# 256-token stages of a two-block transformer kernel: the high and low parts of the activations as one 512-column matmul

## The chip, the cores and the metric

The kernel runs on one core of a Trainium2 chip, in one launch. The metric is device time in microseconds (us). Weights come from HBM on every execution and are used once.

The core's engines have in-order queues and meet through semaphores: PE (matrix multiply), DVE (vector), ACT (scalar, with activation functions), POOL (GpSimd) and SP (here it only issues DMAs). PEld in the profile is PE loading its stationary operand, which overlaps the matmul before.

## The reference, cut to what matters

Two transformer blocks of width 1024 on 256 tokens. The second block runs two layers; it puts 16 meta tokens in front, so its first layer works on 272 tokens, and its second layer again on the 256.

```python
y = jnp.square(jax.nn.relu(h2 @ w_mlp_in[l])) @ w_mlp_out[l]      # block 1: 1024 -> 4096 -> 1024
x = x + gate2[:, None, :] * y
...
def swiglu(h, w_gate, w_up, w_down):                               # block 2: 1024 -> 2816 -> 1024
    return (jax.nn.silu(h @ w_gate) * (h @ w_up)) @ w_down
...
for l in range(DEPTH_2):                                           # two layers, two swiglu each
    h = h + 0.5 * swiglu(rmsnorm_2(h, ffn1_norm[l]), ffn1_w_gate[l], ffn1_w_up[l], ffn1_w_down[l])
    ...
    h = h + 0.5 * swiglu(rmsnorm_2(h, ffn2_norm[l]), ffn2_w_gate[l], ffn2_w_up[l], ffn2_w_down[l])
```

Everything is float32.

## The kernel before

**Splitting.** PE works on `float32r`, a shortened float. So that nothing is lost, every operand is split into a high part and a rest: `hi` is the value rounded by ACT, `lo = value - hi` is made by DVE. A product is then three matmuls, written by `mm3` (lines 116 to 121): high weight with high activation, high weight with low activation, low weight with high activation, all summed into the same columns of a PSUM bank. This text calls the three a triple. Each of the three loads its own stationary weight tile of 128x128.

**Weights.** A weight block is 1 MB, 128 partitions by 2048 values. `ld` (line 82) issues its DMA into one of 3 `raw` buffers, and splits it in two halves of 1024 columns: ACT writes `whi` (line 103), DVE writes `wlo` (line 104). There are 4 `whi` and 4 `wlo` buffers, so two blocks. A half of `whi` can be written when PE has used the half two blocks before it. Half a and half b below are the two halves of one block.

**Activations.** Features lie on partitions, tokens on columns. High and low parts have tiles of their own: `ah` and `al` for the MLP's hidden activations, `gh` and `gl` for those of the FFNs, `yh` and `yl` for the normed input.

**The stages.** `proj` (line 243) walks over weight blocks; one step is one block, two PSUM banks and 16 triples (8 feature tiles of the input by two output tiles). In an FFN, step f gives the gate and the up values of hidden tile f, and `evac` (in `ffn`) takes them out: DVE multiplies the gate sums by the norm's row `R` (line 698), ACT applies Silu (699), DVE multiplies the up sums by `R` (701), POOL multiplies both (702), ACT makes the high part (192) and DVE the low part (193). The first steps wait for `R`, so that their evacuations come together when it lands. `down` (line 627) walks over the second matrix; its evacuation is `devac` (712) or, in block 1, `mlp_out_evac` (648).

The stages on 256 tokens that the change speaks of are the MLP's second matrix in block 1 (4 x 4 blocks) and the two FFNs of the second layer, here called the first and the last 256-token FFN (22 gate/up blocks and 12 down blocks each). In the first of them the projection to the shared latent keys (`latent`) stands behind step 4, two small pieces behind steps 6 and 8.

**Order.** The Tile framework orders the instructions of each engine ahead of time, and each engine then takes its list strictly in order.

Of the kernel before, what the change touches and what calls it, by code (L numbers as in the profile page):

```python
# [18 lines left out]
S = 256  # L19
# [10 lines left out]
# columns of the packed per-feature vectors  # L30
# [15 lines left out]
def net(ctx, tc, d):  # L46
# [35 lines left out]
    def ld(src, n, sub=1024, spare=False, pool=False, cut=False, steps=None, after=((), ())):  # L82
        """parts of a weight block; with steps, the part behind the first is left to a call of what is put there"""
        raw = wp.tile([128, 2048], F32, tag="raw", name=nm("raw"), bufs=3)
        for a, b in ((0, sub), (sub, n)) if cut else ((0, n),):
            with behind(order[:1]):
                i = nc.sync.dma_start(raw[:, a:b], src[:, a:b])
            if order:
                order[:1] = [i]
        parts = []  # L90
        if spare:
            bh, bl = blk([128, 2048], F32R), blk([128, 2048], F32R)

        def part(a):
            m = min(sub, n - a)
            if spare:
                hi, lo = bh[:, a:a + m], bl[:, a:a + m]
            else:
                hi = wp.tile([128, 1024], F32R, tag="whi", name=nm("whi"), bufs=4)
                lo = wp.tile([128, 1024], F32R, tag="wlo", name=nm("wlo"), bufs=4)  # L100
            e = G if pool and a else V
            with behind(after[a > 0]):
                i = A.activation(hi[:, :m], raw[:, a:a + m], AF.Copy)  # L103
                e.tensor_tensor(lo[:, :m], raw[:, a:a + m], hi[:, :m].bitcast(F32), op=OP.subtract)  # L104
            if order and not a:
                order[1:] = [i]
            parts.append((hi, lo))

        for a in range(0, n, sub):
            if a and steps is not None:  # L110
                steps.append(lambda a=a: part(a))
            else:
                part(a)
        return parts

    def mm3(out, w, c0, xh, xl, start, stop, m=128):
        """out += (whi + wlo).T (xhi + xlo), the weights stationary."""
# [3 lines left out]
        TE.matmul(out, lo[:, c0:c0 + m], xh, start=False, stop=stop, skip_group_check=True)  # L121

# [88 lines left out]
    def sumsq_late(parts, src, f, n, sumsq=sumsq):  # L211
        """as sumsq, the last two tiles on their own: their squares are ready sooner."""
# [10 lines left out]
    def proj(src, evac, nj, n, yh, yl, first=2, hooks=(), at={}, orders=(range(0, 6), range(6, KD)), spare=(),  # L223
             after={}):
        """two feature tiles by step. The first steps take the tiles of y in the given order, with what is ready
        first in front; the hooks go behind each part of the order and behind the steps that follow, and only
        then the first sums are used. at[j] goes behind step j."""
# [10 lines left out]
        def mms(pp, w, ks, tiles=(0, 1)):  # L238
            for k in ks:
                for i in tiles:  # L240
                    mm3(pp[i][:, 0:n], w[k // 4], (k % 4) * 256 + i * 128, yh[:, k, :], yl[:, k, :],
                        k == 0, k == KD - 1)
# [50 lines left out]
    def ada(ch, t0, t1, early=False):  # L293
        """feature tiles t0, t1 of the modulation: a row of ada_w.T per partition, times silu(c), summed."""
# [12 lines left out]
    def ada_rest(n, early=False):  # L307
        """n more chunks: gate1, scale2, shift2, gate2."""
# [22 lines left out]
    # position bias with its masks, as a Toeplitz table  # L331
# [50 lines left out]
    # q feature tiles (tokens back to front within each half), then k  # L382
# [25 lines left out]
    def scores(fam, half):  # L408
# [22 lines left out]
        if fam == 0:  # L431
            # heads i, i+4, i+1, i+5 of the sinks
# [24 lines left out]
    def values(fam, heads, Sb, rd, mid):  # L457
        PTs, po = [], []

        def tr(j):  # L460
# [7 lines left out]
            PTs.append(work([128, 384], "PT", bufs=3))  # L468
# [74 lines left out]
    # branches, merge  # L543
# [19 lines left out]
    # out projection, residual; y = x1 * g2 * (1 + scale2), with shift2 as two more columns  # L563
# [27 lines left out]
    # MLP  # L591
    ah = [blk([128, 8, S], F32R) for _ in range(4)]
    al = [blk([128, 8, S], F32R) for _ in range(4)]

    def mlp_evac(f, p):
# [17 lines left out]
    # MLP out, residual; final norm of block 1 and first norm of block 2 both applied late  # L613
# [14 lines left out]
    def down(src, kcs, evac, n, ah, al, before=None):  # L628
        for dp in range(4):
# [3 lines left out]
            for c, (k0, nk) in enumerate(kcs):  # L633
                w = ld(src(dp, c), nk * 256)
                for kk in range(nk):
                    k = k0 + kk
                    for i in range(2):
                        mm3(pp[i][:, 0:n], w[kk // 4], (kk % 4) * 256 + i * 128, ah[k // 8][:, k % 8, :],
                            al[k // 8][:, k % 8, :], k == 0, k == kcs[-1][0] + kcs[-1][1] - 1)
# [15 lines left out]
    down(lambda dp, c: d["mlp_out"][dp * 4 + c], [(8 * c, 8) for c in range(4)], mlp_out_evac, S, ah, al,  # L655
# [17 lines left out]
    def rms_of(get, tiles, n):  # L673
        """hooks that leave the norm of y's tokens in a row."""
# [14 lines left out]
    def ffn(idx, yh, yl, rms, h, n, c0, post, kv=False, before=None, **kw):  # L689
        """h[:, c0:] + half of the swiglu of y; post(f, h_f) for each feature tile of the sum."""  # L690
        gh = [blk([128, nk, n], F32R) for _, nk in FC]
        gl = [blk([128, nk, n], F32R) for _, nk in FC]
        hooks, rc = rms
        c1 = T - n if kv else 0

        def evac(f, pg, pu):
            g = work([128, PADW], "t")[:, :n]
# [37 lines left out]
    # layer 0  # L735
# [25 lines left out]
    def window(g, w, l0, l1, E):  # L761
        """sums over 2, 4, 8, 16 tokens back"""
# [54 lines left out]
    # shared keys and values  # L817
# [76 lines left out]
    # layer 1  # L894
# [93 lines left out]
    def mla_values(b, Pb, rd):  # L988
        PTs = []
        po = ps()  # L990
        for j in range(2):
# [7 lines left out]
            PT = work([128, 384], "PT", bufs=3)  # L999
# [18 lines left out]
    p3 = post_y(y3, ("ffn2_norm", 8), S)  # L1018
# [20 lines left out]
    # the queries' norms and the scale go with the exponentials  # L1039
# [61 lines left out]
def _layout(i):  # L1101
# [15 lines left out]
    def pairs(w):  # L1117
        """[K, F] -> [F / 256, 128, (K / 128) * 256]"""
# [3 lines left out]
    def tiles(w, c):  # L1122
        """[K, F] -> [128, (F / c) * (K / 128) * c]"""
# [78 lines left out]
```

## Time and profile before

| | |
|---|---|
| median of 3 runs | 1280.71 us (1280.71 to 1281.14) |
| span of the profiled execution, first to last instruction | 1279.0 us |
| what lies around the span, median less span | 1.7 us |
| PE busy | 1240.4 us, 97% of the span |
| DVE busy | 855.1 us, 67% |
| ACT busy | 611.3 us, 48% |
| POOL busy | 363.7 us, 28% |
| granted PE clock, mean | 0.993 of 2.4 GHz |

The busy shares are means over stages with different limits. A row of a timeline gives the start in us from the span's start and the duration of an instruction; recorded durations of one engine overlap a little, since instructions are pipelined, so the pace of an engine is read from starts. The bracket at the end of a row is the idle time ahead of it and what ended it.

### The profile page before, as it was taken

Reading aid. Unit: us, or ns where it says so; the run is one execution under the profiler, and the core shown is the slowest. Engines: PE = TensorE matmul, PEld = TensorE weight load, DVE = VectorE, ACT = ScalarE, POOL = GpSimd, SP = SyncE. Lnnn points to the kernel's source line nnn. Section 1 sums busy time; section 2 is a strip of 40 time slices with the busy share of each in tenths; the row PEclk is TensorE's granted clock in tenths of the full one; section 3 lists DMA queues with packets and bytes.
Section 4 is the critical chain, followed back from the end, with each engine's and each line's share of the span. In section 5 each row is a group of like instructions: output and inputs, shape, how many; then the busy total and the mean of one; then the engine's idle time right before and its main releaser. Section 6 shows DMA issues by size and latency. Waiting matters only on the chain.

```text
span 1279.0 us, 24155 instructions
## 1 busy us (share of the span) xinstructions
PE 1240.4 (97%) x9908; PEld 1213.6 (95%) x9908; DVE 855.1 (67%) x1322; ACT 611.3 (48%) x971; POOL 363.7 (28%) x351
## 2 busy tenths in 40 slices
PE   6999999999999999998899999999999999999997
PEld 4988999999999999998899999999999977999997
DVE  7978778887755766566866666666656577666543
ACT  3366445665444544443444444454444454544442
POOL 4333135331325222223222212222222235222221
PEclk9999999999999999999999999999999999999999
DMA  8957864556664554451455455455555423555551
GB/s 326 331 187 285 307 226 169 198 176 253 210 219 165 168 188 173 159 206 65 165 182 181 165 178 168 166 199 170 193 181 182 132 100 129 183 183 189 169 185 53
DMA packets 37057, 238.63 MB, mean 187 GB/s; under 512 B 4242, under 2 KB 6738, under 8 KB 11731
## 3 DMA queue, kind: packets, MB, share of 16 engines
q1 hardware_dynamic: 36946, 237.10, 52.9%
q8 instruction: 77, 1.26, 0.4%
q14 instruction: 34, 0.27, 0.1%
HBM read 236.01 MB, written 1.07 MB: 185 GB/s over the span
## 4 chain that ended last, share of the span: by engine, by line
PE 86%; DVE 7%; issue 3%; POOL 2%; ACT 2%; POOLq 0%; DVEq 0%; ACTq 0%
PE ps L121 27%; PE ps L120 27%; PE ps L119 27%; DVE wlo L104 2%; DVE blk L302 1%; DVE blk L189 1%; POOL blk L341 1%; DVE blk L768 1%; POOL t L561 1%; PE ps L477 1%; PE ps L150 1%; PE ps L467 0%; ACT whi L103 0%; PE ps L175 0%; PE ps L523 0%
## 5 line engine op out<-in xcount | busy, mean ns | idle before, releaser
L121 PE MATMUL ps<-blk,wlo 128*128 128x256 f32 (+2 forms) x3080 | 878.3, 286 | 9.6 <-DVE wlo L104 6.2
L120 PE MATMUL ps<-blk,whi 128*128 128x256 f32 (+2 forms) x3080 | 879.4, 286 | 2.9 <-DVE blk L361 1.8
L119 PE MATMUL ps<-blk,whi 128*128 128x256 f32 (+2 forms) x3080 | 871.1, 286 | 7.6 <-ACT blk L188 4.3
L104 DVE TENSOR_TENSOR wlo<-raw,whi 128x1024 fp32r<-128x1024 f32 (+2 forms) x395 | 485.8, 1233 | 248.0 <-ACT whi L103 247.5
L121 PEld LDWEIGHTS ps<-blk,wlo 128*128 128x128 f32 x3080 | 588.3, 191 | 11.8 <-DVE wlo L104 7.4
L119 PEld LDWEIGHTS ps<-blk,whi 128*128 128x128 f32 x3080 | 585.8, 192 | 10.0 <-ACT blk L188 4.5
L120 PEld LDWEIGHTS ps<-blk,whi 128*128 128x128 f32 x3080 | 588.6, 191 | 3.8 <-DVE blk L361 2.3
L103 ACT ACTIVATE whi<-raw 128x1024 fp32r<-128x1024 f32 (+3 forms) x403 | 412.5, 1030 | 364.4 <-PE ps L120 339.3
L702 POOL TENSOR_TENSOR u<-u,t 128x272 f32<-128x272 f32 (+1 forms) x88 | 117.5, 1336 | 349.0 <-ACT t L699 344.7
L192 ACT ACTIVATE blk<-u 128x272 fp32r<-128x272 f32 (+1 forms) x88 | 37.2, 424 | 129.6 <-POOL u L702 129.6
L193 DVE TENSOR_TENSOR blk<-u,blk 128x272 fp32r<-128x272 f32 (+1 forms) x88 | 39.1, 446 | 83.5 <-ACT blk L192 83.5
L200 POOL TENSOR_TENSOR sq<-blk 128x256 f32<-128x256 f32 (+1 forms) x45 | 36.7, 817 | 129.1 <-DVE blk L712 124.8
L201 POOL TENSOR_TENSOR ss<-ss,sq 128x256 f32<-128x256 f32 (+1 forms) x52 | 64.5, 1243 | 3.5
L698 DVE TENSOR_TENSOR t<-ps,R 128x272 f32<-128x272 f32 (+1 forms) x88 | 37.8, 429 | 10.4 <-POOL u L702 5.9
L603 POOL TENSOR_TENSOR q<-u 128x256 f32<-128x256 f32 x32 | 28.3, 901 | 54.6 <-ACT u L601 54.2
L189 DVE SCALAR_TENSOR_TENSOR blk<-blk,vec,blk 128x272 fp32r<-128x272 f32 (+1 forms) x48 | 38.4, 844 | 0.2 <-ACT blk L188 0.2
L699 ACT ACTIVATE t<-t 128x272 f32<-128x272 f32 (+1 forms) x88 | 35.8, 410 | 5.3 <-DVE t L698 4.9
L701 DVE TENSOR_TENSOR u<-ps,R 128x272 f32<-128x272 f32 (+1 forms) x88 | 37.8, 429 | 0.1
L302 DVE SCALAR_TENSOR_TENSOR raw<-raw,csb 128x1024 f32<-128x1024 f32 x30 | 36.8, 1250 | 1.5 <-DMA raw<-in_ada_w 1.5
L168 POOL TENSOR_TENSOR col<-col,mhalf 128x2 f32<-128x2 f32 (+1 forms) x12 | 12.2, 1020 | 80.5 <-DVE col L161 70.8
L188 ACT ACTIVATE blk<-blk,vec 128x272 fp32r<-128x272 f32 (+1 forms) x48 | 22.1, 507 | 26.1 <-DVE blk L774 14.0
L302 DVE SCALAR_TENSOR_TENSOR blk<-blk,csb 128x1024 f32<-128x1024 f32 x18 | 32.0, 1813 | 1.4 <-DMA blk<-in_ada_w 1.4
(213 smaller groups left out, 695.5 us busy)
## 6 DMA issues: line engine op xcount, KB each, us to landing
raw<-in_f_gu SPq DMA_DIRECT2D x88, 1024.0 KB, 4.9
raw<-in_f_down SPq DMA_DIRECT2D x32, 1024.0 KB, 4.9
raw<-in_mlp_in SPq DMA_DIRECT2D x16, 1024.0 KB, 4.9
raw<-in_mlp_out SPq DMA_DIRECT2D x16, 1024.0 KB, 5.3
raw<-in_ada_w SPq DMA_DIRECT2D x15, 1024.0 KB, 5.1
raw<-in_f_down SPq DMA_DIRECT2D x16, 768.0 KB, 4.3
blk<-in_ada_w SPq DMA_DIRECT2D x9, 1024.0 KB, 8.9
raw<-in_w_gate SPq DMA_DIRECT2D x7, 1024.0 KB, 5.0
```

What stands on the lines that cost most here:

```text
L103: i = A.activation(hi[:, :m], raw[:, a:a + m], AF.Copy)
L104: e.tensor_tensor(lo[:, :m], raw[:, a:a + m], hi[:, :m].bitcast(F32), op=OP.subtract)
L119: TE.matmul(out, hi[:, c0:c0 + m], xh, start=start, stop=False, skip_group_check=True)
L120: TE.matmul(out, hi[:, c0:c0 + m], xl, start=False, stop=False, skip_group_check=True)
L121: TE.matmul(out, lo[:, c0:c0 + m], xh, start=False, stop=stop, skip_group_check=True)
L189: return V.scalar_tensor_tensor(lo, src, g, hi.bitcast(F32), op0=OP.mult, op1=OP.subtract)
L193: V.tensor_tensor(lo, src, hi.bitcast(F32), op=OP.subtract)
L201: G.tensor_tensor(ss, ss, q, op=OP.add)
L302: V.scalar_tensor_tensor(w, w, 1.0, csb, op0=OP.mult, op1=OP.mult, accum_out=mod[:, t:t + 1])
L698: V.tensor_tensor(g, pg[:, 0:n], rc["R"][:, c1:], op=OP.mult)
L701: V.tensor_tensor(u, pu[:, 0:n], rc["R"][:, c1:], op=OP.mult)
L702: G.tensor_tensor(u, u, g, op=OP.mult)
```

## The change

In the three stages named above the high and the low part of an activation tile stand next to each other in one buffer (`Parts`: 4 feature tiles by 2 parts by 256 tokens). `mm2` then passes both, 512 columns, by the weight's high part in one matmul. The result fills a whole PSUM bank: columns 0 to 255 hold what the high part gives, columns 256 to 511 what the low part gives. The weight's low part times the activation's high part is added to columns 0 to 255 as before. So a triple becomes two matmuls, and a triple's two halves are added when the bank is taken out: in gate/up by POOL, after DVE has multiplied all 512 columns by `R`; in the down stages by one more instruction on ACT and one more on DVE. The buffers `PT`, which hold the multiplied halves, are widened from 384 to 512 columns and are 4 in place of 3; the attentions use them too. Stages on 258 and 272 tokens keep `mm3`.

```diff
+    def mm2(p, w, c0, x, k, start, stop):
+        hi, lo = w
+        TE.matmul(p[:, 0:2 * S], hi[:, c0:c0 + 128], x.both(k), start=start, stop=False, skip_group_check=True)
+        TE.matmul(p[:, 0:S], lo[:, c0:c0 + 128], x.hi(k), start=False, stop=stop, skip_group_check=True)
+    class Parts:
+        def __init__(self, nk):
+            self.t = [blk([128, min(4, nk - k), 2, S], F32R) for k in range(0, nk, 4)]
...
-    ah = [blk([128, 8, S], F32R) for _ in range(4)]
-    al = [blk([128, 8, S], F32R) for _ in range(4)]
+    am = Parts(32)
...
     def mlp_out_evac(f, p):
         x2 = work([128, PADW], "t")[:, :S]
-        V.scalar_tensor_tensor(x2, p[:, 0:S], mod[:, GA2 + f:GA2 + f + 1], x1[:, f, :], op0=OP.mult, op1=OP.add)
+        x2l = work([128, PADW], "u")[:, :S]
+        ga = mod[:, GA2 + f:GA2 + f + 1]
+        A.activation(x2l, p[:, S:2 * S], AF.Copy, scale=ga)
+        V.scalar_tensor_tensor(x2, p[:, 0:S], ga, x1[:, f, :], op0=OP.mult, op1=OP.add)
+        V.tensor_tensor(x2, x2, x2l, op=OP.add)
...
+        def evac2(f, pg, pu):
+            Rb = rc["R"][:, None, c1:].to_broadcast([128, 2, S])
+            g2 = work([128, 2 * S], "PT", bufs=4).rearrange("p (a n) -> p a n", a=2)
+            V.tensor_tensor(g2, pg.rearrange("p (a n) -> p a n", a=2), Rb, op=OP.mult)
+            g = work([128, PADW], "t")[:, :n]
+            G.tensor_tensor(g, g2[:, 0], g2[:, 1], op=OP.add)
+            A.activation(g, g, AF.Silu)
+            u2 = work([128, 2 * S], "PT", bufs=4).rearrange("p (a n) -> p a n", a=2)
+            V.tensor_tensor(u2, pu.rearrange("p (a n) -> p a n", a=2), Rb, op=OP.mult)
+            u = work([128, PADW], "u")[:, :n]
+            G.tensor_tensor(u, u2[:, 0], u2[:, 1], op=OP.add)
+            G.tensor_tensor(u, u, g, op=OP.mult)
+            split_act(gh.hi(f), gh.lo(f), u)
...
+            if two:
+                b = work([128, PADW], "u")[:, :n]
+                A.activation(b, p[:, n:2 * n], AF.Copy, scale=0.5)
             split[:] = [V.scalar_tensor_tensor(hn[:, f, :], p[:, 0:n], 0.5, h[:, f, c0:], op0=OP.mult, op1=OP.add)]
+            if two:
+                V.tensor_tensor(hn[:, f, :], hn[:, f, :], b, op=OP.add)
             post(f, hn[:, f, :])
...
-            PT = work([128, 384], "PT", bufs=3)
+            PT = work([128, 2 * S], "PT", bufs=4)[:, 0:384]
```

PE's list in the last FFN, at the start of a gate/up step (`ps` is the bank, `blk` the activation, `whi` and `wlo` the weight's parts), before and then now:

```order
L119 MATMUL ps_13186<-blk_12280,whi_13178 128x256
L120 MATMUL ps_13186<-blk_12281,whi_13178 128x256
L121 MATMUL ps_13186<-blk_12280,wlo_13179 128x256
L119 MATMUL ps_13187<-blk_12280,whi_13178 128x256
L120 MATMUL ps_13187<-blk_12281,whi_13178 128x256
L121 MATMUL ps_13187<-blk_12280,wlo_13179 128x256
```

```order
L126 MATMUL ps_12126<-blk_11632,whi_12118 128x512
L127 MATMUL ps_12126<-blk_11632,wlo_12119 128x256
L126 MATMUL ps_12127<-blk_11632,whi_12118 128x512
L127 MATMUL ps_12127<-blk_11632,wlo_12119 128x256
L126 MATMUL ps_12126<-blk_11632,whi_12118 128x512
```

Lines 119 and 120 became one row of 512 columns. The whole program has 1312 rows of that kind now.

DVE's list in the last FFN, a little over one gate/up step, before and then now (`t` and `u`, or `PT`, take the gate and up sums of step f; `blk<-u,blk` makes the low part of step f; `wlo` with one `raw` number are halves a and b of one block):

```order
L104 TENSOR_TENSOR wlo_13315<-raw_13312,whi_13314 128x1024
L698 TENSOR_TENSOR t_13236<-ps_13186,R_12546 128x256
L701 TENSOR_TENSOR u_13239<-ps_13187,R_12546 128x256
L104 TENSOR_TENSOR wlo_13319<-raw_13312,whi_13318 128x1024
L193 TENSOR_TENSOR blk_12414<-u_13239,blk_12411 128x256
L104 TENSOR_TENSOR wlo_13383<-raw_13380,whi_13382 128x1024
```

```order
L104 TENSOR_TENSOR wlo_12231<-raw_12228,whi_12230 128x1024
L735 TENSOR_TENSOR PT_12160<-ps_12126,R_11866 128x512
L740 TENSOR_TENSOR PT_12165<-ps_12127,R_11866 128x512
L104 TENSOR_TENSOR wlo_12235<-raw_12228,whi_12234 128x1024
L214 TENSOR_TENSOR blk_11763<-u_12167,blk_11763 128x256
L104 TENSOR_TENSOR wlo_12287<-raw_12284,whi_12286 128x1024
```

The places are the same in both: between the gate and up sums of step f and half a of the next block stand half b and the low part of step f. Lines 735 and 740 read 512 columns in place of 256. ACT's list per step is the same in both too: Silu of step f, high part of step f, `whi` half a, `whi` half b.

POOL's list at the start of the last FFN's evacuations, before and then now (`sq` and `ss` belong to the norm ahead, `col` is its power, `t` is the gate, `u` the up value):

```order
L200 TENSOR_TENSOR sq_12405<-blk_11865 128x256
L201 TENSOR_TENSOR ss_12282<-ss_12282,sq_12405 128x256
L168 TENSOR_TENSOR col_12517<-col_12515,mhalf 128x2
L702 TENSOR_TENSOR u_12551<-u_12551,t_12548 128x256
L702 TENSOR_TENSOR u_12559<-u_12559,t_12556 128x256
```

```order
L189 TENSOR_TENSOR col_11845<-col_11843,mhalf 128x2
L737 TENSOR_TENSOR t_11870<-PT_11868 128x256
L742 TENSOR_TENSOR u_11875<-PT_11873 128x256
L737 TENSOR_TENSOR t_11882<-PT_11880 128x256
L742 TENSOR_TENSOR u_11887<-PT_11885 128x256
L743 TENSOR_TENSOR u_11875<-u_11875,t_11870 128x256
L743 TENSOR_TENSOR u_11887<-u_11887,t_11882 128x256
```

Each step has three rows on POOL now, where it had one: the halves of the gate are added (737), those of the up values (742), and the two are multiplied (743).

## Rows read from the trace of the kernel before

**Rows 1.** The page: span, busy time by engine, and the chain that ended last.
```profile
span 1279.0 us, 24155 instructions
...
PE 1240.4 (97%) x9908; PEld 1213.6 (95%) x9908; DVE 855.1 (67%) x1322; ACT 611.3 (48%) x971; POOL 363.7 (28%) x351
...
PE 86%; DVE 7%; issue 3%; POOL 2%; ACT 2%; POOLq 0%; DVEq 0%; ACTq 0%
```

**Rows 2.** Windows: gate/up stage of the last FFN; a stretch with stalls.
```profile
core 0: us, PE busy (x) PEld busy (x) DVE busy (x) ACT busy (x) POOL busy (x), PEclk, DMA share, GB/s
...
1092.00:1207.00 115.00, 115.00 (x961) 115.00 (x960) 72.26 (x105) 56.28 (x83) 28.45 (x21) 1.00 0.53 182
590.00:600.00 10.00, 6.71 (x53) 6.27 (x52) 6.58 (x9) 4.71 (x9) 5.78 (x7) 1.00 0.01 2
```

**Rows 3.** Timeline of PE, last FFN (start us, us, engine, line, operation, tiles).
```profile
1100.07 0.28 PE L121 MATMUL ps<-blk,wlo 128*128 128x256 f32 x1
...
1107.63 0.28 PE L121 MATMUL ps<-blk,wlo 128*128 128x256 f32 x1
```

**Rows 4.** Timeline of PE, second attention: 512-column matmuls, first and last of 17.
```profile
1038.78 0.40 PE L890 MATMUL ps<-wlo,blk 128*128 128x512 f32 x1
...
1042.48 0.40 PE L891 MATMUL ps<-whi,blk 128*128 128x512 f32 x1
```

**Rows 5.** Timeline of DVE, last FFN.
```profile
1097.09 0.42 DVE L698 TENSOR_TENSOR t<-ps,R 128x256 f32<-128x256 f32 x1
...
1097.83 1.23 DVE L104 TENSOR_TENSOR wlo<-raw,whi 128x1024 fp32r<-128x1024 f32 x1
1100.13 0.42 DVE L193 TENSOR_TENSOR blk<-u,blk 128x256 fp32r<-128x256 f32 x1 [1.08 <-ACT blk L192]
1101.08 1.23 DVE L104 TENSOR_TENSOR wlo<-raw,whi 128x1024 fp32r<-128x1024 f32 x1 [0.52 <-ACT whi L103]
1102.22 0.42 DVE L698 TENSOR_TENSOR t<-ps,R 128x256 f32<-128x256 f32 x1
...
1107.95 0.42 DVE L698 TENSOR_TENSOR t<-ps,R 128x256 f32<-128x256 f32 x1
```

**Rows 6.** Timeline of ACT, last FFN.
```profile
1099.68 0.42 ACT L192 ACTIVATE blk<-u 128x256 fp32r<-128x256 f32 x1 [1.59 <-POOL u L702]
1100.01 1.04 ACT L103 ACTIVATE whi<-raw 128x1024 fp32r<-128x1024 f32 x1
1102.43 1.06 ACT L103 ACTIVATE whi<-raw 128x1024 fp32r<-128x1024 f32 x1 [1.38 <-PE ps L120]
```

**Rows 7.** Timeline of POOL, last FFN.
```profile
1093.71 1.45 POOL L702 TENSOR_TENSOR u<-u,t 128x256 f32<-128x256 f32 x2 [4.75 <-ACT t L699]
1098.23 1.42 POOL L702 TENSOR_TENSOR u<-u,t 128x256 f32<-128x256 f32 x1 [3.06 <-ACT t L699]
```

**Rows 8.** Timeline of POOL and then of DVE ahead of the last FFN.
```profile
1074.37 0.61 POOL L200 TENSOR_TENSOR sq<-blk 128x256 f32<-128x256 f32 x1
1075.06 1.60 POOL L201 TENSOR_TENSOR ss<-ss,sq 128x256 f32<-128x256 f32 x1
...
1074.40 1.67 DVE L104 TENSOR_TENSOR wlo<-raw,whi 128x1024 fp32r<-128x1024 f32 x1
```

**Rows 9.** Groups by line and form: DVE reading 256 and 512 columns of PSUM.
```profile
L698 DVE TENSOR_TENSOR t<-ps,R 128x256 f32<-128x256 f32 x44 | 18.4, 419 | 0.6 <-PE ps L121 0.5
...
L892 DVE TENSOR_SCALAR blk<-ps,col 128x512 f32<-128x512 f32 x3 | 2.1, 717 | 0.0
```

**Rows 10.** Line 702: durations of the POOL multiply, min/median/max in ns.
```profile
L702 POOL TENSOR_TENSOR u<-u,t x88: 735/1424/1587, 413.8 to 1207.7; 128x272 f32<-128x272 f32 x44, 128x256 f32<-128x256 f32 x44
```

**Rows 11.** Timeline of ACT, first 256-token FFN, around the latent projection.
```profile
850.82 2.65 ACT L862 COPY blk<-t 32x272 f32<-32x272 f32 x8 [0.41 <-DVE t L860]
```

**Rows 12.** Timeline of DVE at the end of the program.
```profile
1269.23 0.79 DVE L712 SCALAR_TENSOR_TENSOR blk<-ps,blk 128x256 f32<-128x256 f32 x2 [8.42 <-PE ps L121]
```

More of the change, by code (lines that the diff above doesn't have):

```diff
@@ L121, in mm3, with hi, lo, both @@
         TE.matmul(out, lo[:, c0:c0 + m], xh, start=False, stop=stop, skip_group_check=True)
+    def mm2(p, w, c0, x, k, start, stop):
[5 more added lines that the diff above has]
+            self.t = [blk([128, min(4, nk - k), 2, S], F32R) for k in range(0, nk, 4)]
+        def hi(self, k):
+            return self.t[k // 4][:, k % 4, 0, :]
+        def lo(self, k):
+            return self.t[k // 4][:, k % 4, 1, :]
+        def both(self, k):
+            return self.t[k // 4][:, k % 4].rearrange("p a n -> p (a n)")
     def vc(name, i=0, n=1):
@@ L240, in mms @@
                 for i in tiles:
-                    mm3(pp[i][:, 0:n], w[k // 4], (k % 4) * 256 + i * 128, yh[:, k, :], yl[:, k, :],
-                        k == 0, k == KD - 1)
+                    c0 = (k % 4) * 256 + i * 128
+                    if yl is None:
+                        mm2(pp[i], w[k // 4], c0, yh, k, k == 0, k == KD - 1)
+                    else:
+                        mm3(pp[i][:, 0:n], w[k // 4], c0, yh[:, k, :], yl[:, k, :], k == 0, k == KD - 1)
         ws, steps = [], []
@@ L467, in tr @@
                 TE.transpose(p[:, cs], Sb[:, j, cs], ident)
-            PTs.append(work([128, 384], "PT", bufs=3))
+            PTs.append(work([128, 2 * S], "PT", bufs=4)[:, 0:384])
             (V.tensor_copy if j == 3 else A.copy)(PTs[j], p[:, 0:384])
@@ L626, in net, with down @@
     G.tensor_copy(h0[:, :, 0:NM], meta)
-    def down(src, kcs, evac, n, ah, al, before=None):
+    def down(src, kcs, evac, n, ah, al=None, before=None):
         for dp in range(4):
@@ L636, in down @@
                     k = k0 + kk
+                    last = k == kcs[-1][0] + kcs[-1][1] - 1
                     for i in range(2):
-                        mm3(pp[i][:, 0:n], w[kk // 4], (kk % 4) * 256 + i * 128, ah[k // 8][:, k % 8, :],
-                            al[k // 8][:, k % 8, :], k == 0, k == kcs[-1][0] + kcs[-1][1] - 1)
+                        c0 = (kk % 4) * 256 + i * 128
+                        if al is None:
+                            mm2(pp[i], w[kk // 4], c0, ah, k, k == 0, last)
+                        else:
+                            mm3(pp[i][:, 0:n], w[kk // 4], c0, ah[k // 8][:, k % 8, :], al[k // 8][:, k % 8, :],
+                                k == 0, last)
             for i in range(2):
@@ L653, in mlp_out_evac @@
         sumsq(ss2[:, NM:T], xg, f == 0, S)
-    down(lambda dp, c: d["mlp_out"][dp * 4 + c], [(8 * c, 8) for c in range(4)], mlp_out_evac, S, ah, al,
+    down(lambda dp, c: d["mlp_out"][dp * 4 + c], [(8 * c, 8) for c in range(4)], mlp_out_evac, S, am,
          before=lambda dp: ada_rest(1))
@@ L689, in ffn @@
     def ffn(idx, yh, yl, rms, h, n, c0, post, kv=False, before=None, **kw):
-        gh = [blk([128, nk, n], F32R) for _, nk in FC]
-        gl = [blk([128, nk, n], F32R) for _, nk in FC]
+        two = yl is None
+        if two:
+            gh, gl = Parts(22), None
+        else:
+            gh = [blk([128, nk, n], F32R) for _, nk in FC]
+            gl = [blk([128, nk, n], F32R) for _, nk in FC]
         hooks, rc = rms
         c1 = T - n if kv else 0
+        def evac2(f, pg, pu):
[11 more added lines that the diff above has]
+            split_act(gh.hi(f), gh.lo(f), u)
         def evac(f, pg, pu):
+            if two:
+                return evac2(f, pg, pu)
             g = work([128, PADW], "t")[:, :n]
@@ L711, in devac @@
             hn = out[0]
+            if two:
+                b = work([128, PADW], "u")[:, :n]
+                A.activation(b, p[:, n:2 * n], AF.Copy, scale=0.5)
             split[:] = [V.scalar_tensor_tensor(hn[:, f, :], p[:, 0:n], 0.5, h[:, f, c0:], op0=OP.mult, op1=OP.add)]
+            if two:
+                V.tensor_tensor(hn[:, f, :], hn[:, f, :], b, op=OP.add)
             post(f, hn[:, f, :])
@@ L717, in ffn, with make_y, post_y @@
         return out[0]
-    def make_y(n, y):
-        y += [blk([128, KD, n], F32R), blk([128, KD, n], F32R), newss()[:, :n]]
-    def post_y(y, g, n, late=False, sumsq=sumsq):
+    def make_y(n, y, parts=False):
+        if parts:
+            y += [Parts(KD), None, newss()[:, :n]]
+        else:
+            y += [blk([128, KD, n], F32R), blk([128, KD, n], F32R), newss()[:, :n]]
+    def post_y(y, g, n, late=False, sumsq=sumsq, parts=False):
         def post(f, hf):
             if f == 0:
-                make_y(n, y)
+                make_y(n, y, parts)
                 if late:
                     y[2] = [y[2]]
-            split.append(split_scaled(y[0][:, f, :], y[1][:, f, :], hf, vc(g[0], g[1] + f)))
+            yh, yl = (y[0].hi(f), y[0].lo(f)) if parts else (y[0][:, f, :], y[1][:, f, :])
+            split.append(split_scaled(yh, yl, hf, vc(g[0], g[1] + f)))
             if late:
```

10 lines of the change are left out of this document (5 added, 5 removed).

## The prediction

> **What bounds the kernel now.** I read the page first: PE is busy 97% of the span and 86% of the chain that ended last lies on it [rows 1]. A mean over the span does not say that each stage is PE's, so the windows come next: in the gate/up stage of the last FFN PE is busy in all 115 of 115 us, while DVE works 72 us of them and POOL 28 [rows 2]. So there PE sets the pace, and the timeline gives that pace: 63 matmuls of 256 columns start in 1107.63 - 1100.07 = 7.56 us, 0.120 us each [rows 3]. A triple costs 0.360, a step of 16 triples 5.76 us.
>
> What matters for this change is how far the others are from binding. DVE, ACT and POOL form a ring, because DVE's list puts the low part of step f, which comes out of POOL and ACT, ahead of the next weight half. One turn can be followed in the timelines of the three: DVE takes the gate sums at 1097.09 [rows 5]; POOL multiplies from 1098.23 to 1099.65 [rows 7]; ACT makes the high part at 1099.68 and half a of `whi` at 1100.01, until 1101.05 [rows 6]; DVE writes the low part at 1100.13, `wlo` half a at 1101.08, and the next gate sums at 1102.22 [rows 5]. That turn took 5.13 us, under PE's 5.76. The next one takes 1107.95 - 1102.22 = 5.73, and in it ACT sits idle 1.38 us for a release by PE [rows 6]: PE is what holds the ring back. The reader should keep two numbers: the ring has only 0.6 us to spare in each turn, and from POOL's end to the next gate sums it takes 1102.22 - 1099.65 = 2.57 us.
>
> **What PE gains.** 1312 triples change. Each loses a 256-column matmul and makes another one 512 long. The trace has 512-column matmuls with a weight load before each: 16 intervals from 1038.78 to 1042.48, 0.231 us [rows 4]. The new pair then costs 0.231 + 0.120 = 0.351, a gain of 8.7 ns, 11.4 us over all. That is the lower bound I see in rows; the upper one takes it that 256 columns at 2.4 GHz are 0.1067 us, that the 13.3 ns left of the 0.120 belong to each matmul and its load, and that one such part goes: 13.3 ns, 17.5 us. I take 8.7, because it is measured at 512 columns. A new step is 16 x 0.351 = 5.62 us.
>
> By the Trainium skill, "TensorE: Matmul & The Clock Gate", section Back-to-back issue gap, a warm matmul costs its columns at 2.4 GHz and about 2.5 ns; then merging would give 2.5 x 1312 = 3.3 us, and the sum would end 8 us higher. The rows here show 13.3 ns above the columns at 256 and 18 at 512, so I do not use it.
>
> **What the ring loses.** The evacuation on 512 columns adds two POOL additions to each turn and lengthens DVE's multiplications. Prices: DVE reads 256 columns of PSUM in 0.42 us and 512 in 0.72 [rows 9], and I use 0.72. A POOL operation with two inputs takes 0.735 alone, 1.42 in the median [rows 10]. The difference is contention with DVE: in the turn above POOL ran from 1098.23, DVE's `wlo` until 1099.06, and POOL ended 0.59 later, at 1099.65. The other way round, POOL's square ran from 1074.37 for 0.61, until 1074.98; `wlo`, issued at 1074.40, ended at 1076.07, 1.09 after that and not 1.67 of its own work; the POOL addition queued behind ended 0.59 after DVE again [rows 8]. So the two exclude each other, whoever comes first keeps the other out for a whole instruction. A DVE instruction that reads PSUM and one SBUF operand does not do that: two POOL multiplies took 1.45 together [rows 7], 0.73 each, while DVE took sums out of PSUM. (The Trainium skill, "SBUF — State Buffer", section Who interferes with whom, states the lock in this form, for a DVE operation with two SBUF inputs against a GpSimd operation that reads SBUF. These rows agree; the sum goes by the rows.)
>
> Now one turn, from DVE's gate sums at 0. They end at 0.72. POOL adds the gate halves from 0.79 to 1.53. DVE is through with the up sums at about 1.3 and wants `wlo` half b, whose `whi` ACT finished before 1.0; it gets in when POOL lets go at 1.53 and ends 1.09 later, at 2.62. The addition of the up halves ends 0.59 after that, 3.21. The product starts 0.08 later (as between dependent POOL instructions, 1075.06 - 1074.98 [rows 8]) and ends at 4.02; Silu lies beside the up addition. Add 2.57 to the next gate sums: a turn is **6.6 us**. If POOL's two additions run before DVE gets in, `wlo` stands ahead of the product all the same, and the turn is as long.
>
> 6.6 is above PE's new 5.62. So in gate/up PE will wait about 0.97 us in each turn, once the lead is used up. The lead: half a of the block made at 1102.22 is used when PE, which ends a block at 1102.43, has done one more, at 1108.2: 6 us. In the last FFN the evacuations of steps 0 to 2 come together, with nine POOL instructions for three. Following the three lists with the prices above, half a of block 5, which the turn above had ready at 1102.2, is split 2.7 us later, at 1104.9; PE, with three shorter blocks behind it, wants it at about 1107.7. So 2.8 are left. From there 19 turns each bring one block that PE waits for (blocks 6 to 21 of gate/up and the first three of down): 19 x 0.97 - 2.8 = 15.6 us. In the first 256-token FFN the latent projection behind step 4 gives PE 24 triples, some 9 us of other work, but ACT (eight copies, 2.65 us [rows 11]) and DVE have work in it too; I leave 1 us of lead at step 5, and 17 turns. 17 x 0.97 - 1 = 15.5, and 1 more for the two small pieces behind steps 6 and 8, whose POOL power and DVE columns join the ring. Together 32.1 us of waiting.
>
> **The rest.** In the down stages the added ACT and DVE instructions are hidden: a block there takes PE 5.62 us and DVE two splits. MLP out is like that. If that cover were gone, it would cost one DVE operation, 0.42 us, per output tile. Only at the end of the program nothing covers them: DVE evacuates the last two tiles in 0.79 us [rows 12]; with ACT's copy and two additions this takes about 0.6 longer. The wider `PT` costs the attentions nothing that I see. No DMA is added or moved; the `raw` of a block is asked for three blocks ahead.
>
> **Sum.** - 11.4 + 32.1 + 0.6 = + 21.3. The profiled execution's 1279.0 becomes 1300.3, and with the 1.7 us around the span **1302 us**.
>
> **Rivals.**
> 1. *The ring does not bind; faster.* If POOL keeps DVE out through all three of its instructions, `wlo` half b runs beside ACT's work: the product ends at 0.79 + 3 x 0.735 + 0.08 = 3.1 and the turn is 5.7, PE's pace. Then the time is 1280.7 - 11.4 + 0.6 = 1270, with the upper gain 1264. It decides at a turn of 6.0, where 36 turns less the lead cost what PE gains. For it: 0.6 us is not much to be wrong by. Against: DVE got in at the first gap [rows 8], and the product always leaves one. 0.17.
> 2. *The ring is longer.* If each POOL instruction takes nearly what line 702 takes in the median, about 1.35, the turn is 0.79 + 3 x 1.35 + 0.08 + 2.57 = 7.5, PE waits 1.9 us, and 36 turns cost 36 x 1.9 - 3 = 65: 1335. For it: 1.42 is the median. Against: DVE has only one `wlo` to put against three POOL instructions. 0.13.
> 3. *The change does not do what it says on PE:* a 512-column matmul takes as long as two of 256. Then nothing is gained, and PE at 5.76 waits 0.84 a turn: 27.5 + 0.6, 1309. [Rows 4] speak against it. 0.05.
>
> **How the numbers follow.** My forecast has 0.62, and 0.03 is for an end within 0.2%, about what a measurement of this kernel can tell from no change. Its own bounds: the upper PE gain is 6 us lower, of which the longer waits take back 2.5; the full lead of 6 us in both FFNs is 8 lower; together with a turn shorter by 0.2 (7 us) about 1284. Rival 2 sets the upper end, 1336. The range 1284 to 1336 leaves out rival 1 and no change, 0.2. Faster 0.17, same 0.03, slower 0.80.
>
> **What would show it.** In gate/up of both FFNs: PE starts 16 pairs in 5.62 us (0.351 a pair), then waits about 1 us for `wlo` line 104, once per step; DVE's gate sums (line 735) start 6.6 us apart; POOL's line 742 lasts longer than 737 and 743, because `wlo` lies in it; ACT no longer waits for PE there. In MLP out and down PE has no gaps, and gains 8.7 ns a pair. PE idles 15% of a step, and [rows 2] show a granted clock of 1.00 at 6.7 us of work in 10. I am wrong if gaps of PE are missing in gate/up (rival 1), if they are near 2 us (rival 2), or if the clock falls in them.

## The result and the profile after

| | before | after |
|---|---|---|
| median | 1280.71 us (1280.32 to 1281.14, 4 runs) | 1300.42 us (1299.98 to 1302.4, 4 runs) |
| ratio, 95% interval | | 1.0156 (1.0142 to 1.0171) |
| span of the profiled execution | 1279.0 us | 1297.9 us |

The change costs 20 us, and the span of the profiled execution grows by 18.9. The page of after answers to [rows 1] so (span, busy time by engine, chain that ended last by engine):

```profile
span 1297.9 us, 21678 instructions
...
PE 1236.9 (95%) x8596; PEld 1140.4 (88%) x8596; DVE 891.8 (69%) x1346; ACT 617.3 (48%) x995; POOL 443.5 (34%) x439
...
PE 63%; DVE 12%; POOL 12%; issue 8%; ACT 5%; DVEq 0%; ACTq 0%; POOLq 0%
```

PE has 1312 matmuls fewer, and its share of the chain has gone from 86% to 63%; DVE and POOL have taken over most of the rest. Neither of them is near full: a chain that moves from PE to two engines at 69% and 34% points to a ring, in which each waits for the other. The windows of the last FFN's gate/up stage show the same beside [rows 2], where PE was busy in all 115 us:

```profile
1115.00:1225.00 110.00, 101.16 (x558) 84.73 (x557) 69.42 (x85) 46.07 (x67) 51.95 (x50) 1.00 0.46 160
```

PE is idle for 8.84 of 110 us, at a granted clock of 1.00. From 1144 us on, the idle time lies in one place per step. Timeline of PE, last FFN:

```profile
1138.43 0.39 PE L126 MATMUL ps<-blk,whi 128*128 128x512 f32 x1
...
1143.64 0.39 PE L126 MATMUL ps<-blk,whi 128*128 128x512 f32 x1
1144.79 0.39 PE L127 MATMUL ps<-blk,wlo 128*128 128x256 f32 x1 [0.76 <-DVE wlo L104]
1145.01 0.39 PE L126 MATMUL ps<-blk,whi 128*128 128x512 f32 x1
```

A pair is a matmul of 512 columns and its one of 256. Here 15 pairs start in 5.21 us, 0.347 each, and then comes a wait for a half of `wlo`. The ring that brings it, in the timelines of DVE, POOL and ACT (as [rows 5 to 7] for before):

```profile
1131.50 0.68 DVE L735 TENSOR_TENSOR PT<-ps,R 128x512 f32<-128x512 f32 x1
1132.10 0.68 DVE L740 TENSOR_TENSOR PT<-ps,R 128x512 f32<-128x512 f32 x1
1132.69 1.39 DVE L104 TENSOR_TENSOR wlo<-raw,whi 128x1024 fp32r<-128x1024 f32 x1
1135.98 0.43 DVE L214 TENSOR_TENSOR blk<-u,blk 128x256 fp32r<-128x256 f32 x1 [1.90 <-ACT blk L213]
1136.93 1.23 DVE L104 TENSOR_TENSOR wlo<-raw,whi 128x1024 fp32r<-128x1024 f32 x1 [0.52 <-ACT whi L103]
1138.07 0.68 DVE L735 TENSOR_TENSOR PT<-ps,R 128x512 f32<-128x512 f32 x1
...
1144.65 0.68 DVE L735 TENSOR_TENSOR PT<-ps,R 128x512 f32<-128x512 f32 x1
```

```profile
1132.26 0.74 POOL L737 TENSOR_TENSOR t<-PT 128x256 f32<-128x256 f32 x1 [3.34 <-DVE PT L735]
1132.96 1.72 POOL L742 TENSOR_TENSOR u<-PT 128x256 f32<-128x256 f32 x1
1134.76 0.74 POOL L743 TENSOR_TENSOR u<-u,t 128x256 f32<-128x256 f32 x1
```

```profile
1135.53 0.42 ACT L213 ACTIVATE blk<-u 128x256 fp32r<-128x256 f32 x1 [2.08 <-POOL u L743]
1135.86 1.99 ACT L103 ACTIVATE whi<-raw 128x1024 fp32r<-128x1024 f32 x2
```

The gate sums start 6.57 and 6.58 us apart. Read down the brackets: DVE waits 1.90 us for ACT, ACT 2.08 for POOL, POOL 3.34 for DVE. In these steps ACT no longer waits for PE, as it did in [rows 6]. In POOL's three instructions the middle one lasts 1.72 us, the others 0.74: `wlo` half b, issued at 1132.69, lies in it.

The waits of PE on that line, by stretch: first 256-token FFN (800 to 1020 us), then the last one's opening (1080 to 1130) and the rest (1130 to 1300). Columns: us in total, times, longest.

```profile
PE ps L127 <- DVE wlo L104: 10.8, 17, 0.8
...
PE ps L127 <- DVE wlo L104: 2.5, 1, 2.5
...
PE ps L127 <- DVE wlo L104: 10.3, 15, 0.8
```

### The profile page after: what moved, and what is told of

Same layout as the page of the kernel before. It is cut to its first block, busy times and chain, and to the rows that moved or that the text cites. A ratio compares the mean times of both kernels' runs of the same rounds, so it can differ in the third digit from the quotient of the medians.

```text
span 1297.9 us, 21678 instructions
## 1 busy us (share of the span) xinstructions
PE 1236.9 (95%) x8596; PEld 1140.4 (88%) x8596; DVE 891.8 (69%) x1346; ACT 617.3 (48%) x995; POOL 443.5 (34%) x439
## 4 chain that ended last, share of the span: by engine, by line
PE 63%; DVE 12%; POOL 12%; issue 8%; ACT 5%; DVEq 0%; ACTq 0%; POOLq 0%
PE ps L120 14%; PE ps L121 14%; PE ps L119 14%; PE ps L126 10%; PE ps L127 5%; POOL u L742 5%; ACT whi L103 4%; DVE wlo L104 3%; POOL u L743 3%; POOL t L737 2%; DVE PT L735 2%; DVE blk L326 2%; DVE blk L210 1%; POOL t L585 1%; DVE blk L829 1%
## 5 line engine op out<-in xcount | busy, mean ns | idle before, releaser
L104 DVE TENSOR_TENSOR wlo<-raw,whi 128x1024 fp32r<-128x1024 f32 (+2 forms) x395 | 492.2, 1251 | 195.0 <-ACT whi L103 194.1
L121 PE MATMUL ps<-blk,wlo 128*128 128x272 f32 (+2 forms) x1768 | 505.5, 288 | 7.5 <-DVE wlo L104 4.7
L120 PE MATMUL ps<-blk,whi 128*128 128x272 f32 (+2 forms) x1768 | 507.0, 288 | 2.7 <-DVE blk L385 1.8
L119 PE MATMUL ps<-blk,whi 128*128 128x272 f32 (+2 forms) x1768 | 498.1, 287 | 7.6 <-ACT blk L209 4.2
L126 PE MATMUL ps<-blk,whi 128*128 128x512 f32 x1312 | 464.3, 398 | 0.0
L127 PE MATMUL ps<-blk,wlo 128*128 128x256 f32 x1312 | 371.5, 283 | 23.7 <-DVE wlo L104 23.6
L119 PEld LDWEIGHTS ps<-blk,whi 128*128 128x128 f32 x1768 | 333.6, 191 | 10.0 <-ACT blk L209 4.5
L120 PEld LDWEIGHTS ps<-blk,whi 128*128 128x128 f32 x1768 | 336.4, 190 | 3.7 <-DVE blk L385 2.3
L126 PEld LDWEIGHTS ps<-blk,whi 128*128 128x128 f32 x1312 | 246.4, 188 | 58.4 <-DVE blk L210 0.2
L754 POOL TENSOR_TENSOR u<-u,t 128x272 f32<-128x272 f32 x44 | 58.5, 1330 | 168.7 <-ACT t L751 164.4
L737 POOL TENSOR_TENSOR t<-PT 128x256 f32<-128x256 f32 x44 | 33.7, 767 | 137.8 <-DVE PT L735 137.8
L742 POOL TENSOR_TENSOR u<-PT 128x256 f32<-128x256 f32 x44 | 72.1, 1640 | 0.0
L738 ACT ACTIVATE t<-t 128x256 f32<-128x256 f32 x44 | 18.3, 419 | 72.7 <-POOL t L737 72.7
```

The costliest lines, as they stand in the source:

```text
L126: TE.matmul(p[:, 0:2 * S], hi[:, c0:c0 + 128], x.both(k), start=start, stop=False, skip_group_check=True)
L127: TE.matmul(p[:, 0:S], lo[:, c0:c0 + 128], x.hi(k), start=False, stop=stop, skip_group_check=True)
L737: G.tensor_tensor(g, g2[:, 0], g2[:, 1], op=OP.add)
L742: G.tensor_tensor(u, u2[:, 0], u2[:, 1], op=OP.add)
L754: G.tensor_tensor(u, u, g, op=OP.mult)
```

## The experiments

Two theories. **Ring:** PE gains what the pairs say, and the additions on POOL, with `wlo` shut out by them and shutting them out, lengthen the turn of DVE, POOL and ACT beyond PE's step. **Rival:** the cost is PE's own (a 512-column matmul or its bank is dear), or the added instructions cost by their number.

**Down only.** Parts and `mm2` in MLP out and the two down stages, `mm3` and the old evacuation in gate/up.

```diff
-        two = yl is None
+        two = n == S
...
-            if two:
-                return evac2(f, pg, pu)
```

> The 512-column pairs stay in MLP out and in the down stages of the two 256-token FFNs (608 triples); gate/up goes back to three matmuls and to its old evacuation. Ring theory (the loss sits in gate/up alone, in the ring of DVE, POOL and ACT): the 608 pairs gain the 6.7 ns each that the changed kernel's down stages show, 4.1 us: 1276.6, faster than before by 0.3%. Rival A (PE itself or the shared port makes 512-column stages slow wherever they are): 1281 or above.

1275.82 us (ratio 0.9963, 0.9949 to 0.9976; the kernel before had 1280.14 in this measurement). 608 pairs bring 1280.14 - 1275.82 = 4.3 us, 7.1 ns each. So the matmul on 512 columns gains, and the down stages hide their added instructions.

**Additions only.** The kernel before, and POOL adds a tile of zeros to the gate and to the up values in each step of 256 tokens.

```diff
+            if n == S:
+                G.tensor_tensor(g, g, zero, op=OP.add)
...
+            if n == S:
+                G.tensor_tensor(u, u, zero, op=OP.add)
```

> The kernel before, with triples of 256 columns everywhere, and in gate/up of the two 256-token FFNs two more POOL additions per step (zeros added to the gate and to the up values, at the places of the additions of halves); DVE reads 256 columns as before. Ring theory: a turn is 0.42 + 0.07 + 0.735 for the first addition, 1.09 for DVE's weight half b, 0.59, 0.08 + 0.735 for the product, 2.57 back to the next gate sums, 6.3 us against PE's 5.76; 36 turns x 0.54 less the lead of about 5.6 us: 14 us, 1294 (1290 to 1298). Rival A (PE's 512-column form is the cause): 1281, no change. Rival B (POOL work as such is harmless, only DVE's longer reads cost): 1281.

1294.43 us (1.0106, 1.0088 to 1.0124). DVE's gate sums and POOL's additions in its timelines:

```profile
1142.13 0.42 DVE L700 TENSOR_TENSOR t<-ps,R 128x256 f32<-128x256 f32 x1
...
1148.45 0.42 DVE L700 TENSOR_TENSOR t<-ps,R 128x256 f32<-128x256 f32 x1
```

```profile
1142.63 0.75 POOL L702 TENSOR_TENSOR t<-t,zero 128x256 f32<-128x256 f32 x1 [3.08 <-DVE t L700]
1143.33 1.73 POOL L707 TENSOR_TENSOR u<-u,zero 128x256 f32<-128x256 f32 x1
1145.13 0.74 POOL L708 TENSOR_TENSOR u<-u,t 128x256 f32<-128x256 f32 x1
```

A turn of 6.32 us with the old matmuls: two POOL additions alone, on an unchanged PE, push the ring past PE's 5.76. The other 0.25 of after's 6.57 is what DVE's longer read of the gate sums would add (0.68 in place of 0.42).

**Low part deferred, and both deferred.** The change as it is, with the low part of step f queued on DVE behind the sums of step f+1; in the second kernel ACT's high part too stands behind step f+1's Silu. `behind` puts what it holds behind the given instructions in the list. Nothing is left out.

```diff
+        held = []
+        def release(*ins):
+            if held:
+                with behind(ins):
+                    split_act(*held.pop())
...
-            A.activation(g, g, AF.Silu)
+            silu = A.activation(g, g, AF.Silu)
...
-            V.tensor_tensor(u2, pu.rearrange("p (a n) -> p a n", a=2), Rb, op=OP.mult)
+            i = V.tensor_tensor(u2, pu.rearrange("p (a n) -> p a n", a=2), Rb, op=OP.mult)
+            release(i, silu)
...
-            split_act(gh.hi(f), gh.lo(f), u)
+            held.append((gh.hi(f), gh.lo(f), u))
...
+        release()
```

(The first kernel has `release(i)`, so only the low part is tied to DVE's sums.)

> The changed kernel; in gate/up the low part of step f, on DVE, is put behind the gate and up sums of step f+1; the high part, on ACT, stays ahead of the weight half a. Ring theory: the ring still closes through ACT (product, high part, whi half a, wlo half a, next gate sums), so a turn stays at 6.6 or a little more and the time at 1300 (1296 to 1305). Rival C (DVE waiting in order for the low part is the whole cause): PE's pace, 1272.

1298.54 us (1.0142, 1.0121 to 1.0163). The ring closes through ACT: its `whi` of the next block stands behind the high part, which waits for POOL. Timeline of ACT, then of DVE:

```profile
1146.52 0.42 ACT L213 ACTIVATE blk<-u 128x256 fp32r<-128x256 f32 x1 [2.14 <-POOL u L750]
```

```profile
1147.92 1.23 DVE L104 TENSOR_TENSOR wlo<-raw,whi 128x1024 fp32r<-128x1024 f32 x1 [2.02 <-ACT whi L103]
```

DVE's wait has only changed its name, from the high part's to `whi`'s; a turn takes 6.63 us.

> The changed kernel; in gate/up the high part on ACT and the low part on DVE of step f both go behind Silu and the sums of step f+1. No work is taken away. Ring theory: the ring is cut, a turn needs about 5.1 us, PE's 5.65 sets the pace again; all 1312 pairs gain 6.7 ns, 8.8 us: 1272.5 (1270 to 1275), faster than before and than the changed kernel. Rival B (POOL's load, or the exclusion between POOL and DVE, binds in whatever order): 1290 or more.

1272.42 us (0.9934, 0.9912 to 0.9957), faster than both kernels; profiled span 1268.3. DVE's gate sums now wait for PE:

```profile
1141.38 0.69 DVE L741 TENSOR_TENSOR PT<-ps,R 128x512 f32<-128x512 f32 x1 [0.22 <-PE ps L127]
...
1146.92 0.69 DVE L741 TENSOR_TENSOR PT<-ps,R 128x512 f32<-128x512 f32 x1 [0.22 <-PE ps L127]
```

5.54 us a turn is PE's step, and PE is busy in 110.00 of 110 us (1115 to 1225). The counts of instructions are those of after on PE, DVE, ACT and POOL (8596, 1346, 995, 439), in another order, and the time is 28 us less: the loss is all in the order. POOL's up addition still lasts 1.71 us beside `wlo`; it only no longer stands on the way to the next gate sums.

**The later split on the kernel before,** as a control: the same edit, with three matmuls a triple.

> The kernel before with the later split of each gate/up step, and with three matmuls per triple. PE theory: its ring was already under PE's pace, so nothing is gained: 1280.7, within 0.2%. Rival (the later split is worth something by itself, and the gain of both deferred is not the merged matmul's): about 1272.

1280.8 us (1.0, 0.9991 to 1.0009). Where PE binds, the deferral is worth nothing.

**Additions on DVE.** The two `G.tensor_tensor(..., op=OP.add)` of `evac2` become `V.tensor_tensor`.

> DVE adds the halves itself; POOL keeps only the product. Ring theory, prices of the trace of after: gate sums start at 0, up sums at 0.60, the two additions (0.35 from start to start, as line 214 at 0.43 less its overlap) start at about 1.25 and 1.6, the half b of wlo at 1.95. It starts before POOL's product can, so the product ends 0.59 after it: 1.95 + 1.15 + 0.59 = 3.7, and the next gate sums come 2.57 later: a turn of 6.25 us, PE waits 0.6 a turn instead of 0.92, and the time is about 1290 (1283 to 1296). Rival (POOL's extra instructions as such are the cost): the ring is back under PE's pace and the time is about 1272.

1284.72 us (1.0029, 1.002 to 1.0039). DVE's timeline, one turn:

```profile
1134.38 0.68 DVE L735 TENSOR_TENSOR PT<-ps,R 128x512 f32<-128x512 f32 x1
...
1136.25 1.22 DVE L104 TENSOR_TENSOR wlo<-raw,whi 128x1024 fp32r<-128x1024 f32 x1
...
1140.64 0.69 DVE L735 TENSOR_TENSOR PT<-ps,R 128x512 f32<-128x512 f32 x1
```

The turn is 6.26 us, as expected; the time is at the lower end because the ring binds later. PE waits for `wlo` in 8 steps of the first FFN and 12 of the last, where I had taken nearly all 36. The profile shows at most 0.2 us of idle time in each of them, though a step of PE takes 6.25 us there and 5.55 to 5.65 ahead of them: the bracket shows only part of what a wait costs.

**Half b later.** `wlo` half b queued on DVE behind the low part, out of POOL's way (`after=((), los[-2:-1])` in `proj`'s `ld`, with `los` the low parts made so far).

> DVE's half b of wlo is queued behind the low part of the step, so that no subtraction with two SBUF inputs runs beside POOL's three instructions; nothing is removed. Exclusion theory: POOL's line for the addition of the up halves falls from 1.72 to 0.74 us, the product ends at 0.76 + 3 x 0.74 + 0.1 = 3.05, and from there the low part, two halves of wlo (1.15 each) and ACT's high part stand before the next gate sums, 3.2 us: a turn of 6.25, time about 1289 (1283 to 1295). Rival (the 1.72 us are POOL's own wait for the sums or its own work): that line stays near 1.7, the turn is 7.2, the time about 1325.

1295.64 us (1.0113, 1.0098 to 1.0129). POOL's timeline, one turn:

```profile
1137.85 0.74 POOL L739 TENSOR_TENSOR t<-PT 128x256 f32<-128x256 f32 x1 [3.86 <-DVE PT L737]
1138.55 0.74 POOL L744 TENSOR_TENSOR u<-PT 128x256 f32<-128x256 f32 x1
1139.37 0.73 POOL L745 TENSOR_TENSOR u<-u,t 128x256 f32<-128x256 f32 x1
1143.97 0.74 POOL L739 TENSOR_TENSOR t<-PT 128x256 f32<-128x256 f32 x1 [3.87 <-DVE PT L737]
```

With no `wlo` beside it the up addition takes 0.74 in place of 1.72: about 1 us of the 1.72 was DVE's. By the Trainium skill, "SBUF — State Buffer", section Who interferes with whom, a DVE operation with two SBUF inputs and a GpSimd operation that reads SBUF shut each other out; these rows agree. The turn is 6.12 us (6.25 expected). Of the 1 us that POOL gets back the ring loses 0.5 again, because half b now stands on it behind the low part: from the product's end (1140.10) to the next gate sums (1143.20) it is 3.10 us, where after takes 2.57. The time missed: at 1295.64 it lies just above my 1283 to 1295. The forced order also has waits where the stages open: idle time of 4.5 us for `wlo` and 1.5 for `whi` from 1070 to 1120 us, of which both deferred has 2.5, and of 2.2 and 1.3 from 820 to 880, where both deferred has none.

**Grouped.** Both deferred, and in gate/up the two output tiles of a feature tile go 512, 512, 256, 256.

```diff
...
+                    for i, c0 in cs:
+                        TE.matmul(pp[i][:, 0:2 * S], hi[:, c0:c0 + 128], yh.both(k), start=k == 0, stop=False,
+                                  skip_group_check=True)
+                    for i, c0 in cs:
+                        TE.matmul(pp[i][:, 0:S], lo[:, c0:c0 + 128], yh.hi(k), start=False, stop=k == KD - 1,
+                                  skip_group_check=True)
```

> Both splits deferred, and in gate/up the matmuls of the two output tiles go in the order 512, 512, 256, 256 columns instead of 512, 256, 512, 256. If each matmul has its own price whatever stands beside it, the pair stays at 0.347 to 0.353 us and the time at 1272.4 (1270 to 1275). If what a pair takes above its columns comes from the change of length or from how loads and matmuls fall together, the 704 pairs of the two gate/up stages move by some 7 ns each: about 5 us, to 1267 or 1277.

1266.21 us (0.989, 0.9875 to 0.9905), the lowest median here, though the groups of eight below are not clear of it. PE's timelines, both deferred and then grouped, each in the first 256-token FFN and in the last:

```profile
899.77 0.40 PE L126 MATMUL ps<-blk,whi 128*128 128x512 f32 x1
...
911.79 0.40 PE L126 MATMUL ps<-blk,whi 128*128 128x512 f32 x1
...
1129.74 0.39 PE L126 MATMUL ps<-blk,whi 128*128 128x512 f32 x1
...
1141.87 0.40 PE L126 MATMUL ps<-blk,whi 128*128 128x512 f32 x1
```

```profile
900.10 0.63 PE L265 MATMUL ps<-blk,whi 128*128 128x512 f32 x2
...
911.25 0.63 PE L265 MATMUL ps<-blk,whi 128*128 128x512 f32 x2
...
1129.61 0.63 PE L265 MATMUL ps<-blk,whi 128*128 128x512 f32 x2
...
1141.46 0.63 PE L265 MATMUL ps<-blk,whi 128*128 128x512 f32 x2
```

In the order 512, 256 a pair takes 12.02 / 34 = 0.3535 us in one stage and 12.13 / 35 = 0.3466 in the other; grouped it takes 11.15 / 32 and 11.85 / 34, 0.348 in both. So grouping gains 5 ns a pair in the first FFN and loses 2 in the profiled last one, some 1.1 us together. The two profiled executions differ by 3.3 us. From the first to the last pair the first FFN takes 198.18 us in both deferred and 195.27 in grouped: beside the gate/up pairs, its down stage goes at 0.3533 a pair in the one and 0.3466 in the other, with the same list, another 1.2 us. The medians differ by 6.2; the rest is not accounted for.

**Grouped everywhere, and groups of eight.** The same order in MLP out and the down stages too; and, apart from that, in gate/up eight matmuls of 512 of one weight half ahead of its eight of 256.

> As grouped, and the order 512, 512, 256, 256 in MLP out and in the two down stages too. In the run of grouped a pair took 0.348 us where it was grouped, against 0.353 in its MLP out in the order 512, 256. If the order alone sets the pair, the 256 pairs of MLP out gain 5 ns each, 1.3 us, and the 352 of the down stages between nothing and 1.8 us: about 1264 (1263 to 1266). Rival (the pair has two paces whatever the order, and what comes before a stage picks one): MLP out keeps 0.353 or the stages keep what they had, 1266.

1269.98 us (0.992, 0.9902 to 0.9937): not 1264. Its MLP out does take 0.349 a pair (eight pairs from 299.68 to 302.47 us) and is 1.4 us shorter than that of grouped, as expected; the down stages, which had 0.3466 in grouped, take 0.348 and gain nothing. In the profiled execution the time was given back behind MLP out: from its last pair to the first pair of the first 256-token FFN it is 427.4 us, in grouped 423.9. PE ran on to the norm's sum before POOL had the squares, and then had a lower granted clock. PE's timeline and the windows:

```profile
394.62 0.83 PE L171 MATMUL ps<-ones,ss 128*128 128x4 f32 x6 [1.52 <-POOL ss L222]
```

```profile
393.00:398.00 5.00, 3.48 (x22) 3.39 (x23) 1.02 (x6) 0.41 (x1) 3.16 (x4) 0.81 0.62 213
398.00:403.00 5.00, 5.00 (x36) 5.00 (x36) 2.45 (x2) 1.70 (x2) 0.00 (x0) 0.85 0.00 0
403.00:408.00 5.00, 5.00 (x41) 4.85 (x41) 2.12 (x2) 2.78 (x4) 0.06 (x1) 1.00 0.62 210
```

In 10 us PE did 22 + 36 = 58 matmuls here, and 43 + 42 in the same windows of grouped, where it did not wait and the clock was 1.00. The 0.81 and 0.85 are means over both levels of the clock: the matmuls of 272 columns start 0.227 us apart from 396.16 to 399.11 us, at 1.2 GHz, and 0.13 us apart ahead of it and behind, at 2.4. The wait of 1.5 us and these matmuls, some 1.4 us, are most of the 3.5 lost. That the wait brought the clock down is likely and was not tried, nor whether the other executions had both.

> As grouped, but in gate/up eight matmuls of 512 columns of one weight half follow each other, then its eight of 256. If each matmul has its price by its length, a pair costs 0.231 + 0.120 = 0.351 as in the rows of before, 3 ns more than grouped by two, and the time is about 1268. If the change of length costs, there are four times fewer of them and the pair falls below 0.347: 1264 or less.

1267.73 us (0.9905, 0.9887 to 0.9923). PE's timeline:

```profile
900.91 2.00 PE L266 MATMUL ps<-blk,whi 128*128 128x512 f32 x8
902.75 1.12 PE L269 MATMUL ps<-blk,wlo 128*128 128x256 f32 x8
903.70 2.00 PE L266 MATMUL ps<-blk,whi 128*128 128x512 f32 x8
```

Eight of 512 take 1.84 us, eight of 256 take 0.95: 0.349 a pair. With four times fewer changes of length the pair costs no less than in grouped (0.348), so a change of length has no price that shows here; each matmul has about the price of its length in [rows 3, 4].

## Why the prediction was right

The forecast was 1302 us, the measurement 1300.42. By its steps:

- **PE's gain, 8.7 ns a pair, 11.4 us.** The mechanism is right, the size holds in the sum and not in the parts: 13 ns in gate/up of after's last FFN (0.347, above), but 6.7 in its MLP out, 12 pairs at 0.3533 by PE's timeline:

```profile
299.66 0.40 PE L126 MATMUL ps<-blk,whi 128*128 128x512 f32 x1
...
303.90 0.40 PE L126 MATMUL ps<-blk,whi 128*128 128x512 f32 x1
```

  The other stages of after go at 0.353 too, so 960 pairs at 6.7 ns and 352 at 13 make 11.0 us. That two errors nearly cancel is luck. The rival that a 512-column matmul gains nothing is refuted by this and by down only. The other price the prediction weighed, about 2.5 ns a merged triple (the Trainium skill, "TensorE: Matmul & The Clock Gate", section Back-to-back issue gap, where it belongs to the spacing of an isolated matmul), is below the gain at either pace that the runs show.
- **The turn, 6.6 us.** Measured 6.57, and each station stands in the rows above, from the gate sums at 1131.50: gate addition until 1.50 (1.53 predicted), `wlo` until 2.58 (2.62), up addition until 3.18 (3.21), product until 4.00 (4.02), and 2.57 to the next gate sums (2.57). The sums themselves take 0.68, not 0.72.
- **PE's wait, 0.97 a turn.** The turn less 16 pairs is 6.57 - 16 x 0.3535 = 0.91 in the first FFN, where 15 pairs of after start between 925.01 and 930.31 us, and 6.57 - 16 x 0.347 = 1.02 in the last. The profile puts 0.64 to 0.77 of it down as idle; the matmuls around the gap take the rest.
- **How often.** First FFN: 17 turns predicted, and 17 waits found, two of them early and short (0.30 and 0.47 us idle). Last FFN: 19 turns less a lead of 2.8 us, or 16 full waits, predicted; 15 found, and one of 2.5 us in its opening, which before and both deferred have too. Both deferred has the same matmuls and no ring, so the stages of the two give the cost: from the first to the last pair the first FFN takes 213.84 us in after and 198.18 in both deferred, the last 203.63 and 188.37. That is 15.7 and 15.3 us more; 1.2 of the latter is the down stage, which goes at 0.353 a pair in after and 0.347 in both deferred. The waits cost 29.8 us against 32.1. The leads of 1 and 2.8 us and the 1 us for the small pieces were rough allowances; that they came out so near is partly luck.
- **The tail, 0.6.** From the last block of transposes (PE's timelines, before and after) to the end of the span it was 1279.0 - 1269.39 = 9.61 and is 1297.9 - 1287.63 = 10.27: 0.66.

```profile
1269.39 1.47 PE L1078 MATMUL ps<-ident,blk 128*128 128x128 f32 x12
```

```profile
1287.63 1.47 PE L1139 MATMUL ps<-ident,blk 128*128 128x128 f32 x12
```

- **The down stages** hide their extra instructions: PE has no wait for `wlo` in MLP out of after, and down only gains there.
- **The clock** did not fall in the gaps of gate/up (1.00). The row that the prediction took for this, 590 to 600 us in [rows 2], was thin ground: in the kernel before, the next 10 us, with PE busy 7.16, had 0.83:

```profile
600.00:610.00 10.00, 7.16 (x41) 6.77 (x42) 9.90 (x15) 6.68 (x12) 6.15 (x5) 0.83 0.00 0
```

So -11.0 + 29.8 + 0.7 = +19.5, against 21.3 predicted and 18.9 measured: the waits were 2.3 us too dear, the gain 0.4 too large. The 0.6 left lies outside these stages; MLP out, for one, starts 0.8 us earlier in after. That the ring doesn't bind (1270) would have needed DVE to be kept out through all three POOL instructions; the up addition of 1.72 us shows that it got in. That each POOL instruction takes its median of before (1335) was wrong for the reason given: there is one `wlo` to meet three of them.

## What to carry to other kernels

Before PE is made faster, follow one turn of the engines that feed it: a ring with 0.6 us to spare turned a gain of 11 us (by the paces; 8 by the medians of before and both deferred) into a loss of 20, though DVE was 67% and POOL 28% busy. When an in-order ring binds, look first at the order: queueing the dependent split one step later on both engines, with not an instruction less, brought back 28 us and left the gain, while doing it on one of them brought 2 at most, within the intervals of the two ratios. And a stage that ends sooner may only arrive early at its next wait, as grouped everywhere did at the norm's sum in the profiled execution.

## What the hardware showed that I had not expected

One list of alternating 512- and 256-column matmuls has two paces, 0.3535 and 0.3466 us a pair, within one execution (both deferred, rows above), both at a granted clock of 1.00. The order 512, 512, 256, 256 gave 0.348 to 0.349 in every stage where it stood. What picks the pace was not settled: the down stage of the first FFN has the same list in both deferred and in grouped, and goes at 0.3533 in the one and 0.3466 in the other. The runs of both deferred lie between 1270.08 and 1275.25 us, those of before, in the same measurement, between 1279.33 and 1284.17; whether the two paces have a part in such spreads was not tried.
